# One unit of q, not two, in the first modulation's stage of a hybrid GLA and Fourier step, with two more modulation granules beside GLA and fewer on TensorE

## The chip, the cores and the metric

One core of one Trainium2 chip runs the whole kernel. The metric is the device time of one execution in microseconds (us), the median of several runs. Smaller is better.

## The reference

One layer of a diffusion backbone over 128 context tokens and 256 latent tokens (384 in all, D = 2048), everything in float32. What matters here:

```python
mod = jax.nn.silu(cond) @ lw['w_ada'] + lw['b_ada']          # D x 6D, two conditions
sh1, sc1, ga1, sh2, sc2, ga2 = jnp.split(mod, 6)
h = rmsnorm(x, norm_pre_mix) * (1.0 + sc1) + sh1
m, s_f, s_b = mixer(h, ...)                                  # proj = h @ w_in: q, k, v, gate, ...
x = x + ga1 * rmsnorm(m, norm_post_mix)
h = rmsnorm(x, norm_pre_ffn) * (1.0 + sc2) + sh2
ff = (silu(h @ w_ffn_gate) * (h @ w_ffn_up)) @ w_ffn_down
x = x + ga2 * rmsnorm(ff, norm_post_ffn)
```

The mixer runs gated linear attention (GLA, four heads, q and k of 128 columns a head, v of 256) in two directions, a two-dimensional DFT branch, and merges both with sigmoid gates of `h`.

## The kernel before

Activations lie transposed (channels on partitions, 384 tokens in the free dimension). For accuracy, each float32 operand of a large product is split into two parts of type fp32r, `hi` (a copy on ACT) and `lo` (a subtraction on DVE), and each product is three matmuls: hi·hi, hi·lo, lo·hi. Weights come in *granules* of 128x1024 (512 KB): SP issues the transfer to `raw` (L234), ACT makes `whi` (L300), DVE makes `wlo` (L287). `proj` (L348 on) computes one *unit* (128 output columns for 384 tokens): two *half units* of 24 matmuls each (L326). After each half it takes a step of the work that runs beside it, by a generator.

The stages around the change, in order of time:

**First stage** (L529 on, sixteen turns `kb` of one loop, one for each block of 128 channels). Turn `kb` makes shift and scale of block `kb` from two 1 MB slabs of `w_ada` (`gemv`, L474, 32 instructions), turns them to columns (L595), makes `h` of that block (DVE and ACT, L583 to L379), and, a turn behind, computes v of the block before it (`vprod`, L491, three times 6 matmuls) and `XU` units of q (`xprod`, L509, 3 matmuls each). The products of a turn are added to SBUF accumulators by DVE (`flush`, L504). From turn 3 the second q unit uses the PSUM bank `pgm`, which `gemv` also writes. Each turn loads one `w_v` granule (512 KB), `w_x` (128 rows of `XU`x128 floats, 128 KB here) and the two slabs, all for the turn after it. SP issues them in program order; the `raw` buffers (two) come free with DVE's `wlo` (L297). Turn 4 also loads five small tables (L457 to L461).

**GLA stage.** The other q and k units (`qk_order`), then 25 units of the merge gates (`GF`). Beside each half unit, `side` (L969) takes one step of `gla()` (L779) and one of `ada`, the modulation of the other parts. `gla()` for head 0 has some empty steps (`if h == 0: yield`). Its PE work: scores `at` (L875) need `ki` of DVE (L852) of the step before; state updates `dl` (L788) need the split of `ko` (L379, `part`) of the step before.

**Modulation granules** (`ada_rest`, L685). For m = 2, 3, 4 and two halves of 1024 columns: sixteen granules of `w_ada` (512 KB, issued by POOL, two buffers `adaw`) and then one step without work, one with PE's selection products (L718), one with the turn to columns. A granule is computed in one of two ways. On DVE: two operations of 128x1024 (L705 for the first, L707). On PE (`on_pe[0]` true): four products with the 128x32 stationary `spad` (L697), eight instructions in the trace. The last granules run beside `w_out`.

**Mix stage.** Eight `o` units (two halves each), sixteen Fourier units `b` (`four`), and sixteen `a` units (24 matmuls, L326, `pmm<-o_hi`), in `mix_order`. `side` (L1179) counts half units of `o` in `turn` and takes modulation steps there; each `a` unit in the table `TAIL` takes one step ahead of its product, on PE where the table says True. An `a` unit's product is merged by DVE (L1296, L1297) and split to `mT` (L379, `A_lo`). Then `w_out` reads `mT`.

In the trace before, PE does ten granules: at `turn` 7, 9, 11, 13, 15 and in `a` units 1, 5, 8, 11, 13.

Of the kernel before, what the change touches and what calls it, by code (L numbers as in the profile page):

```python
# [25 lines left out]
T = TC + TL  # L26
# [8 lines left out]
FC = 4  # L35
NFC = FT // FC
G = 1024
XU = 2
GF = 25
GD = 256  # L40
TAIL = {1: True, 4: False, 5: True, 8: True, 10: False, 11: True, 13: True, 14: False, 15: False}


C_TRI = 0
# [63 lines left out]
def tile_step(ctx: ExitStack, tc: tile.TileContext, a, o):  # L108
# [49 lines left out]
    srcs = [a["w_v"][k] for k in range(KT)]  # L158
    qk_order = [i for i in (4, 5, *range(XU, 4), 6, 7)]
    for i in qk_order:  # L160
# [250 lines left out]
    with ExitStack() as s:  # L411
# [11 lines left out]
        def load_w(kb):  # L423
            load()
            xraw[kb] = pb.tile([P, XU * P], F32, tag="xraw", name="xraw", bufs=2)
            SP.dma_start(xraw[kb], a["w_x"][kb])
# [39 lines left out]
        pgm = pss.tile([P, 512], F32, tag="side", name="pgm")  # L466
        pgv, pmod = pgm[:, 0:256], pgm[:, 256:512]
        px = pss.tile([P, T], F32, tag="side", name="px")
# [37 lines left out]
        def xprod(u, kb, w, bank=px):  # L506
            def mm():
                for j, (x_, w_) in enumerate(passes(w)):
                    PE.matmul(bank, w_[:, u * P : (u + 1) * P], hT[x_][:, kb, :], start=j == 0, stop=j == 2)  # L509

            return mm, lambda dst=None: flush(xacc[u], kb == 0, dst, bank)
# [38 lines left out]
        prev = None  # L550
        for kb in range(KT):
            if kb and kb + 1 < KT:
                load_slab(kb + 1)
                load_w(kb + 1)
                if kb == 4:
                    load_later()

            wait = kb in (1, 2)
            if kb and not wait:
                gemv(kb)  # L560
            todo = []
            if kb > 4 and kb % 4 == 2:
                todo.append(lrprod(kb - 6))

            both = kb > 2
            if both:
                xs = [xprod(u, kb - 1, prev[1], bank) for u, bank in enumerate((px, pgm[:, 0:T]))]
            elif kb:
                todo += [xprod(u, kb - 1, prev[1]) for u in range(XU)]
            todo += [None] * (4 - len(todo))  # L570
            flushes = [t[1] if t else lambda: None for t in todo]

            def pe_x(n):
                if todo[n]:
                    todo[n][0]()

            if wait:
                vprod(kb - 1, prev[0], (0,))
            pe_x(0)
            hf = scr[:, kb % 8, :]  # L580

            xr = hf if kb else qs[0]
            DVE.tensor_mul(xr, xn(kb), rstd if kb else px)  # L583
            flushes[0]()
            if wait:
                gemv(kb)
            if kb:
                ev = pb.tile([P, 256], F32, tag="ev", name="ev")
                ACT.copy(ev, pgv)
            lag = []  # L590
            new = split_w(kb, lag)
            if kb:
                vprod(kb - 1, prev[0], (1 if wait else 0,))
            for m in range(2):
                PE.transpose(pmod[:, m * P : (m + 1) * P], ev[:, m * P : (m + 1) * P], ident)  # L595
            if kb == 0:

                for _ in range(6):
                    PE.matmul(pv[5][:, 0:P], ones, ones, start=True, stop=True)
            pe_x(1)  # L600

            pm = pb.tile([P, 2, 2], F32, tag="pm", name="pm", bufs=2)
            DVE.tensor_reduce(
                pm, pmod.rearrange("p (m q r) -> p m r q", m=2, q=4)[:, :, 0:2, :], axis=mybir.AxisListType.X, op=ALU.add,
            )
            DVE.tensor_scalar(
                mods[:, 1, kb, :], pm[:, 1, :], bsc1[:, 0, kb : kb + 1], norms[:, 0, kb : kb + 1],
                op0=ALU.add, op1=ALU.mult,
            )
            DVE.tensor_scalar_add(mods[:, 0, kb, :], pm[:, 0, :], cols[:, 0, kb : kb + 1])  # L610
            for lo, hi, c in segs:
                DVE.tensor_scalar(
                    hf[:, lo:hi], xr[:, lo:hi], mods[:, 1, kb, c : c + 1], mods[:, 0, kb, c : c + 1],
                    op0=ALU.mult, op1=ALU.add,
                )
                if kb == 0:
                    ACT.activation(
                        hT[0][:, kb, lo:hi], xr[:, lo:hi], AF.Identity,
                        bias=mods[:, 0, kb, c : c + 1], scale=mods[:, 1, kb, c : c + 1],
                    )  # L620
            flushes[1]()
            if kb:
                split_act(hT[0][:, kb, :], hT[1][:, kb, :], hf)
            else:
                ACT.copy(rstd, px)
                DVE.tensor_sub(hT[1][:, kb, :], hf, hT[0][:, kb, :].bitcast(F32))
            if kb:
                if not wait:
                    vprod(kb - 1, prev[0], (1,))
                pe_x(2)  # L630
                flushes[2]()
            if both:
                for mm, _ in xs:
                    mm()
                for _, fl in reversed(xs):
                    fl()
            for sub in lag:
                sub()
            if kb:
                vprod(kb - 1, prev[0], (2,))  # L640
                pe_x(3)
                flushes[3]()
            prev = new
# [39 lines left out]
    on_pe = [False]  # L683
# [69 lines left out]
    with ExitStack() as s:  # L753
# [25 lines left out]
        def gla():  # L779
# [10 lines left out]
            for h in range(NH):  # L790
# [38 lines left out]
                for d in range(2):  # L829


                    bT = pss.tile([P, T], F32, tag="side", name="bT")
                    for t in range(3):
                        for j, l in enumerate((lah, lal)):
                            PE.matmul(
                                bT[:, t * P : (t + 1) * P], l[:, t, d], tri[:, d * P : (d + 1) * P],
                                start=j == 0, stop=j == 1,
                            )
                    sx = pss.tile([P, 2, P], F32, tag="side", name="sx")
                    for j, l in enumerate((lah, lal)):  # L840
                        PE.matmul(
                            sx, tri[:, (2 + d) * P : (3 + d) * P], l[:, 0 : 2 + d : 1 + d, d], start=j == 0, stop=j == 1,
                        )
                    eb = pg.tile([P, T], F32, tag=f"eb{d}", name="eb")
                    ACT.activation(eb, bT, AF.Exp)
                    ki = pg.tile([P, T], F32, tag=f"ki{d}", name="ki")
                    ACT.activation(ki, bT, AF.Exp, scale=-1.0)
                    ko = pg.tile([P, 2, P], F32, tag=f"ko{d}", name="ko")
                    ACT.activation(ko, sx, AF.Exp)
                    qi = pg.tile([P, T], F32, tag=f"qi{d}", name="qi")  # L850
                    DVE.scalar_tensor_tensor(qi, eb, DK**-0.5, qT[:, h, :], op0=ALU.mult, op1=ALU.mult)
                    DVE.tensor_mul(ki, ki, kT[:, h, :])  # L852
                    DVE.tensor_mul(ko, ko, krs[:, 0 : 2 + d : 1 + d, :])

                    last = 0 if d else CH - 1
                    tot = chunks(eb)[:, :, d, last : last + 1]
                    kc = pg.tile([P, 3, CH], F32, tag=f"kc{d}", name="kc")
                    DVE.tensor_mul(kc, chunks(ki)[:, :, d, :], tot.to_broadcast([P, 3, CH]))
                    dc = pg.tile([P, 1], F32, tag=f"dc{d}", name="dc")
                    c = 5 if d else 2  # L860
                    e0, e1 = c * CH + last, (c + 1 - 2 * d) * CH + last
                    DVE.tensor_mul(dc, eb[:, e0 : e0 + 1], eb[:, e1 : e1 + 1])
                    qin.append(qi)
                    kin.append(ki)
                    kcr.append(kc)
                    kout.append(ko)
                    dec.append((tot, dc))
                    yield

                ats = []  # L870
# [128 lines left out]
    px = fs.enter_context(tc.tile_pool(name="px", bufs=1))  # L999
# [93 lines left out]
    with ExitStack() as s:  # L1093
# [83 lines left out]
        turn = [0]  # L1177

        def side():  # L1179
            while True:  # L1180
                on_pe[0] = turn[0] > 6 and turn[0] != 8
                if turn[0] < 9 or turn[0] % 2:
                    next(ada_gen, None)
                on_pe[0] = False
                turn[0] += 1
                next(df, None)
                next(nw, None)
                yield
# [121 lines left out]
    with ExitStack() as s:  # L1310
# [94 lines left out]
        u = pd.tile([P, 2, 3], F32, name="u12", bufs=1)  # L1405
# [355 lines left out]
        bank = {}  # L1761
# [69 lines left out]
        for kind, c, i in steps[:-4]:  # L1831
# [8 lines left out]
            if kind == "D":  # L1840
# [9 lines left out]
                h = hid_last if last_c else hid  # L1850
# [248 lines left out]
```

## Time and profile before

| | |
|---|---|
| median of 3 runs | 1942.72 us (1942.26 to 1943.35) |
| the profiled execution | 1942.28 us |
| its span, first to last instruction | 1940.4 us |
| granted TensorE clock, mean | 0.998 |
| first stage, about | 0 to 142 us |
| GLA stage | 142 to 456 us |
| mix stage, `o` / `a` and `b` | 537 to 651 / 651 to 733 us |
| `w_out` | 733 to 869 us |
| FFN | 886 us to the end |

Times in the profile are microseconds from the first instruction unless marked ns. PE is TensorE's matmul, PEld its weight load, DVE VectorE, ACT ScalarE, POOL GpSimd, SP the engine that issues most transfers ("q" behind a name: its sequencer). L707 is line 707 of the kernel. A matmul's busy time overlaps with that of the next one, so the pace of PE is read from the starts of its instructions, or from the chain of waits, not from their durations.

### The profile page before, as it was taken

To read this page: it belongs to the slowest core of one execution; us is meant where nothing else is said; L and a number is where in the kernel's file an instruction comes from. 1 tells how busy PE (TensorE), PEld (TensorE's weight loads), DVE (VectorE), ACT (ScalarE), POOL (GpSimd) and SP (SyncE) were. 2 spreads that over 40 slices of the span, in tenths; PEclk is the share of its full clock that TensorE was granted. 3 is DMA by queue.
4 is the path that set the end of the run, shared out by engine and by line. 5 is a ranking of instruction groups with operands and counts; after the bars stand their busy time and mean duration, and the time that the engine had idled before them with its cause. 6 is when DMAs were issued, how large, how long until landed. Compare 5 with 4: busy or idle time off the path is not lost.

```text
span 1940.4 us, 27538 instructions
## 1 busy us (share of the span) xinstructions
PE 1920.4 (99%) x10534; PEld 1690.8 (87%) x10534; DVE 1647.8 (85%) x2172; ACT 916.3 (47%) x1298; POOL 85.8 (4%) x154
## 2 busy tenths in 40 slices
PE   9999999999999999999999999999999999999997
PEld 5779999999999999999988888888888888888886
DVE  5668898889878887978789888999998999888885
ACT  4235455545456554456455444444444444444444
POOL 0001111100000000104000000000000000000001
PEclk9999999999999999999999999999999999999999
DMA  9977766766757885755264636363636272625243
GB/s 390 387 260 248 240 234 227 248 231 194 225 185 246 302 302 181 245 193 198 83 195 131 200 103 194 121 211 98 216 104 213 91 222 93 201 76 185 87 173 110
DMA packets 200615, 380.52 MB, mean 196 GB/s; under 512 B 14196, under 2 KB 126932, under 8 KB 196132
## 3 DMA queue, kind: packets, MB, share of 16 engines
q1 hardware_dynamic: 181252, 320.84, 48.9%
q0 software_dynamic: 13952, 50.39, 8.5%
q10 hardware_dynamic: 5280, 7.55, 1.1%
q8 instruction: 82, 1.34, 0.3%
q14 instruction: 49, 0.40, 0.1%
HBM read 361.94 MB, written 16.78 MB: 195 GB/s over the span
## 4 chain that ended last, share of the span: by engine, by line
PE 93%; DVE 3%; DMA 2%; issue 1%; ACT 1%; SPq 0%; DVEq 0%; ACTq 0%
PE pgu L338 30%; PE pmm L326 30%; PE pdn L338 18%; PE pv L491 3%; PE pgm L474 1%; PE pf L1239 1%; PE pfo L1039 1%; DVE adacc L707 1%; PE pmm L1516 1%; PE ptr L1808 1%; PE pf L1240 1%; PE pfo L1040 1%; DMA xraw<-in_w_x 1%; PE po L788 1%; PE px L509 0%
## 5 line engine op out<-in xcount | busy, mean ns | idle before, releaser
L326 PE MATMUL pmm<-A_hi,whi 128*128 128x384 f32 x1072 | 361.7, 337 | 0.0
L326 PE MATMUL pmm<-A_hi,wlo 128*128 128x384 f32 x1072 | 358.8, 335 | 0.0
L326 PE MATMUL pmm<-A_lo,whi 128*128 128x384 f32 x1072 | 358.6, 335 | 0.0
L1663 ACT CAST whi<-u 128x1024 fp32r<-128x1024 f32 x200 | 210.6, 1053 | 281.5 <-DVE u L1647 86.5
L1663 ACT CAST whi<-raw 128x1024 fp32r<-128x1024 f32 x175 | 184.2, 1052 | 200.8 <-PE pgu L338 63.8
L1674 DVE TENSOR_TENSOR wlo<-u,whi 128x1024 fp32r<-128x1024 f32 x200 | 244.1, 1220 | 32.0 <-ACT whi L1663 18.3
L338 PE MATMUL pgu<-whi,A_hi 128*128 128x512 f32 x640 | 250.0, 391 | 0.0
L338 PE MATMUL pgu<-whi,A_lo 128*128 128x512 f32 x640 | 249.3, 389 | 0.0
L1674 DVE TENSOR_TENSOR wlo<-raw,whi 128x1024 fp32r<-128x1024 f32 x175 | 213.4, 1220 | 34.6 <-ACT whi L1663 25.6
L287 DVE TENSOR_TENSOR wlo<-raw,whi 128x1024 fp32r<-128x1024 f32 x163 | 198.2, 1220 | 24.1 <-ACT whi L300 23.7
L300 ACT CAST whi<-raw 128x1024 fp32r<-128x1024 f32 x149 | 156.0, 1051 | 117.6 <-PE pmm L326 50.0
L326 PEld LDWEIGHTS pmm<-A_hi,whi 128*128 128x128 f32 x1072 | 201.2, 188 | 3.3 <-issue 2.5
L326 PEld LDWEIGHTS pmm<-A_lo,whi 128*128 128x128 f32 x1072 | 201.4, 188 | 0.2
L326 PEld LDWEIGHTS pmm<-A_hi,wlo 128*128 128x128 f32 x1072 | 201.2, 188 | 0.3 <-DVE wlo L287 0.2
L707 DVE SCALAR_TENSOR_TENSOR adacc<-adaw,spad,adacc 128x1024 f32<-128x1024 f32 x160 | 198.1, 1279 | 3.5 <-DMA adaw<-in_w_ada 3.2
L338 PE MATMUL pdn<-whi,hid_hi 128*128 128x512 f32 x480 | 186.9, 389 | 0.0
L338 PE MATMUL pdn<-whi,hid_lo 128*128 128x512 f32 x480 | 186.8, 389 | 0.0
L338 PE MATMUL pgu<-wlo,A_hi 128*128 128x512 f32 x640 | 184.2, 389 | 0.0
L338 PEld LDWEIGHTS pgu<-whi,A_hi 128*128 128x128 f32 x640 | 120.2, 188 | 26.1 <-issue 0.8
L338 PEld LDWEIGHTS pgu<-wlo,A_hi 128*128 128x128 f32 x640 | 120.1, 188 | 25.4
L338 PEld LDWEIGHTS pgu<-whi,A_lo 128*128 128x128 f32 x640 | 120.1, 188 | 25.0
L338 PE MATMUL pgu<-whi,S 128*128 128x512 f32 x480 | 131.1, 395 | 0.0
(405 smaller groups left out, 3042.7 us busy)
## 6 DMA issues: line engine op xcount, KB each, us to landing
adaw<-in_w_ada POOLq DMA_DIRECT2D x96, 512.0 KB, 4.0
raw<-in_w_d SPq DMA_DIRECT2D x88, 512.0 KB, 3.7
slab<-in_w_ada SPq DMA_DIRECT2D x32, 1024.0 KB, 10.2
raw<-in_w_gate SPq DMA_DIRECT2D x64, 512.0 KB, 4.4
raw<-in_w_g SPq DMA_DIRECT2D x48, 512.0 KB, 3.4
raw<-in_w_u SPq DMA_DIRECT2D x48, 512.0 KB, 3.5
raw<-in_w_in SPq DMA_DIRECT2D x44, 512.0 KB, 4.3
u<-in_w_u SPq DMA_DIRECT2D x40, 512.0 KB, 4.6
```

Of the source, the lines that this page charges most:

```text
L287: eng.tensor_sub(lo, raw, hi.bitcast(F32))
L300: ACT.copy(hi, raw)
L326: PE.matmul(dst, w[wi][:, k * n + n0 : k * n + n0 + P], x[xi][:, k0 + k, :], start=first and k == 0 and j == 0, stop=last and k == kts - 1 ...
L338: PE.matmul(dst, stat[x_][m], mov(w[w_], m), start=first and w_ == m == x_ == 0, stop=last and w_ == m == 1,)
L474: PE.matmul(pgv[q : q + 32, :], spad[:, k, :], slab[k // (KT // 2)][:, k % (KT // 2), :], start=k < 4, stop=k >= KT - 4,)
L491: PE.matmul(pv[2 * t + g], hT[x_][:, kb, t * P : (t + 1) * P], w_[:, g * 512 : (g + 1) * 512], start=kb == 0 and j == 0, stop=kb == KT - 1 ...
L707: DVE.scalar_tensor_tensor(acc[:, c, :], w, spad[:, k, c : c + 1], acc[:, c, :], op0=ALU.mult, op1=ALU.add,)
L788: PE.matmul(dst, w[wi], x[xi], start=first and j == 0, stop=last and j == 2)
L1039: PE.matmul(p, w_of[0][:, i, k, g, :], x[:, :, lo:hi], start=kt == 0, stop=False)
L1040: PE.matmul(p[:, 0], w_of[1][:, i, k, g, :], x[:, 0, lo:hi], start=False, stop=kt == KT - 1)
L1663: ACT.copy(hi, src)
L1674: DVE.tensor_sub(lo, src, hi.bitcast(F32))
```

## The change

```diff
-XU = 2
+XU = 1
 GF = 25
 GD = 256
-TAIL = {1: True, 4: False, 5: True, 8: True, 10: False, 11: True, 13: True, 14: False, 15: False}
+TAIL = {4: False, 8: False, 10: False, 11: False, 13: False, 14: False, 15: False}
...
             if both:
-                xs = [xprod(u, kb - 1, prev[1], bank) for u, bank in enumerate((px, pgm[:, 0:T]))]
+                xs = [xprod(u, kb - 1, prev[1], bank) for u, bank in enumerate((px, pgm[:, 0:T])[:XU])]
...
                     dec.append((tot, dc))
+                    yield
+                if h == 0:
                     yield
...
         def side():
             while True:
-                on_pe[0] = turn[0] > 6 and turn[0] != 8
+                on_pe[0] = turn[0] > 8
                 if turn[0] < 9 or turn[0] % 2:
                     next(ada_gen, None)
```

- The first stage computes unit 0 of q alone. `w_x` is 64 KB a turn, and `pgm` is no longer used for q.
- Unit 1 of q becomes an ordinary unit of the GLA stage (`qk_order` is 4, 5, 1, 2, 3, 6, 7). Its two half units take two steps of `ada`, both granules on DVE, and two of `gla()`.
- Head 0 of `gla()` has one more empty step, between the decays of the second direction and the scores.
- The `a` units take seven modulation steps, not nine, and none of them on PE; `turn` 7 takes its granule on DVE.
- Counted through, PE does granules at `turn` 9, 11, 13 and 15 alone, four in place of ten, and DVE 92 in place of 86. From `w_out` on both kernels take the same steps.

## The prediction

> **What bounds the kernel now.** I read the page first, then the chain of waits, then the stages that the change touches.
>
> ```profile
> PE 1920.4 (99%) x10534; PEld 1690.8 (87%) x10534; DVE 1647.8 (85%) x2172; ACT 916.3 (47%) x1298; POOL 85.8 (4%) x154
> PE 93%; DVE 3%; DMA 2%; issue 1%; ACT 1%; SPq 0%; DVEq 0%; ACTq 0%
> ```
>
> The chain that ends last runs over PE for 93% of the span. So an instruction taken from PE's stream is worth its pace, unless another engine or a transfer then comes last. DVE (85%) and the transfers are the candidates, each in its own stage.
>
> In the first stage the chain of one turn, in order of time (start, us, what), is this; the two rows on top are from turn 1:
>
> ```profile
> 28.03 0.52 ACT A_hi L378
> 28.57 0.56 DVE A_lo L379
> ...
> 105.65 1.86 PE pgm L474 x32
> 107.52 1.59 PE pv L491 x6
> 109.10 0.22 PE pgm L595 x2
> 109.32 1.39 PE pv L491 x6
> 110.71 0.52 PE px L509 x3
> 111.23 0.52 PE pgm L509 x3
> 111.75 1.39 PE pv L491 x6
> 113.14 1.86 PE pgm L474 x32
> ```
>
> PE works through, 113.14 - 105.65 = 7.49 us a turn, and 0.52 us of it are the second q unit (the row `pgm L509`). Turn 1 alone hangs on ACT and DVE. The transfers are close behind, though. The windows' last two columns are the DMA engines' busy share and GB/s; the later rows are the issue of a pair of slabs and their use in the timeline, the landing times of the slabs issued between 90 and 135 us, SP's longest wait, and, for 44 to 62 us, the weight load that waited for a slab:
>
> ```profile
> 30.00:40.00 10.00, 9.78 (x92) 6.17 (x91) 5.86 (x14) 3.29 (x6) 0.00 (x0) 1.00 1.03 416
> 60.00:80.00 20.00, 20.00 (x163) 14.25 (x156) 12.07 (x31) 6.00 (x11) 0.00 (x0) 1.00 1.02 415
> 100.00:110.00 10.00, 10.00 (x74) 7.52 (x71) 5.23 (x14) 3.76 (x7) 0.00 (x0) 1.00 0.96 334
> 110.00:120.00 10.00, 10.00 (x72) 7.68 (x71) 6.58 (x17) 2.65 (x5) 0.00 (x0) 1.00 0.98 363
> ...
> 99.92 0.86 SPq L419 DMA_DIRECT2D slab<-in_w_ada  x2
> 113.08 1.93 PE L474 MATMUL pgm<-slab,spad 128*32 128x256 f32 x32
> ...
> DMA to landing us min/median/max: 9.2/9.9/10.6
> ...
> SPq L234 <- DVE wlo L297: 84.9, 15, 7.2
> ...
>   PEld pgm L474: 0.3, 1
> ```
>
> A turn moves 2 x 1.049 + 0.524 + 0.131 = 2.75 MB. At 415 GB/s that is 6.6 us, under PE's 7.49. SP waits 84.9 us for DVE to free the `raw` buffers, so the loop paces the transfers, not they the loop. Late in the stage the slabs land at 99.92 + 9.9 = 109.8 and are used at 113.08, 3.3 us later. But around turn 6, after SP was held up by the five small tables, a weight load of PE's did wait 0.3 us for a slab: there the margin is gone already.
>
> **The change part by part.**
>
> *The q unit leaves the first stage.* Sixteen products of 0.52 us leave. That of turn 1 gains nothing (ACT and DVE come last there); the others give 15 x 0.52 = 7.8 us. Turn 2 had one wait for the split of `w_x`,
>
> ```profile
> 30.66 0.44 PE L509 MATMUL px<-A_hi,wlo 128*128 128x384 f32 x1 [0.22 <-DVE wlo L440]
> ```
>
> and half that width saves some 0.1 us. Against it stands turn 6. PE gets there 4 x 0.52 = 2.1 us earlier, while the slab comes earlier only by the bytes saved: six half `w_x`, 0.39 MB at 416 GB/s, 0.9 us. The missing 1.2 us become a wait (bounds: 0, as the slot waits of SP may move too; 2.1 if the slab does not move at all). Later turns need 2.69 MB / 415 = 6.5 us against 6.97 and fall back behind PE. Sum: 7.8 + 0.1 - 1.2 = **-6.7** us.
>
> *It comes back as two half units in the GLA stage.* The chain has a pair of half units there as
>
> ```profile
> 242.50 8.32 PE pmm L326 x48
> ```
>
> **+8.3** us. The 1 MB of granules that it loads falls where the DMA engines are 70% busy; its DVE work is below.
>
> *PE granules.* Ten become four. The mix stage shows the price, as its groups of three `a` units with and without a PE granule stand side by side (first column: length in us; third: DVE busy):
>
> ```profile
> 658.08:670.67 12.59, 12.59 (x77) 12.59 (x73) 10.78 (x20) 6.03 (x10) 0.53 (x1) 1.00 0.98 369
> 673.05:686.37 13.32, 13.32 (x82) 12.66 (x81) 12.41 (x21) 6.41 (x11) 1.04 (x2) 1.00 0.91 312
> 688.75:702.08 13.33, 13.33 (x82) 12.67 (x81) 10.21 (x19) 6.42 (x11) 0.53 (x1) 1.00 0.87 296
> 704.46:717.79 13.33, 13.33 (x83) 12.67 (x81) 12.42 (x21) 6.41 (x11) 1.05 (x2) 1.00 0.82 289
> 720.83:750.15 29.32, 29.32 (x172) 29.07 (x168) 22.75 (x31) 13.26 (x20) 2.11 (x4) 1.00 0.69 233
> ...
> 677.35 0.64 PE L697 MATMUL pr<-adaw,spad 128*32 128x256 f32 x8
> ```
>
> 13.32 - 12.59 = 0.73 us for each of `a` 5, 8 and 11 (the instructions and the change of form around them). The three others (`turn` 7, `a` 1, `a` 13) stand next to other small products; I take 0.66. Sum: 3 x 0.73 + 3 x 0.66 = **-4.2** us (bounds: 6 x 0.57 = 3.4 from the granule's first instruction to the next, 677.35 to 677.92; 6 x 0.73 = 4.4).
>
> *The wait in head 0 of GLA.* This is the one place after the first stage where the chain leaves PE for DVE:
>
> ```profile
> 178.97 1.22 DVE L287 TENSOR_TENSOR wlo<-raw,whi 128x1024 fp32r<-128x1024 f32 x1
> 180.10 2.47 DVE L707 SCALAR_TENSOR_TENSOR adacc<-adaw,spad,adacc 128x1024 f32<-128x1024 f32 x2
> 182.49 1.21 DVE L287 TENSOR_TENSOR wlo<-raw,whi 128x1024 fp32r<-128x1024 f32 x1
> ...
> 191.34 0.57 PE L875 MATMUL at<-qi,ki 128*64 128x64 f32 x12
> ...
> 193.46 0.57 PE L875 MATMUL at<-qi,ki 128*64 128x64 f32 x12 [1.55 <-DVE ki L852]
> ...
> 210.49 0.75 DVE L379 TENSOR_TENSOR part<-ko,part 128x256 fp32r<-128x256 f32 x2
> 211.22 0.88 PE L788 MATMUL dl<-vr,part 128*128 128x256 f32 x6
> ```
>
> DVE is full from 152 us and behind: the second half of `at` waits, some 1.7 us in PE's pace. The added empty step puts `at` one half unit (4.2 us) later, past `ki`. What is late next is `dl`. An empty step still costs DVE a weight split and a granule, 182.49 - 178.97 = 3.5 us. The first `part` is ready at 210.49 + 0.4 and moves to 214.4; PE, without the old wait, reaches `dl` at 211.22 - 1.7 + 4.2 = 213.7. So about 0.8 us of the wait return there: **-0.9** us (bounds: -1.7, all gone; 0, all moved). Behind `dl` stand only more half units. The two steps of `ada` without DVE work follow directly, so DVE catches up.
>
> *DVE in the mix stage.* Granules of 2.4 us are new on DVE at `turn` 7 and at `a` 8, 11 and 13. From 658 us on DVE has 1.8, 0.9, 3.1 and 0.9 us free in the four groups above, and some 1.5 of the 6.6 free in the last window lie ahead of `a` 14 (an estimate); PE gets 3.5 us faster up to `w_out`. DVE's last split for `w_out` is now
>
> ```profile
> 736.47 1.23 DVE L379 TENSOR_TENSOR A_lo<-yb,A_hi 128x384 fp32r<-128x384 f32 x2
> ```
>
> and ends at 737.7. The granules at `a` 8, 11 and 13 add 7.2 us, of which the free time up to there (0.9 + 3.1 + 0.9 + 1.5) takes 6.4: some 738.5. `w_out`'s second half ends at 720.83 + 29.32 x 5/7 = 741.8 now and reads that split 0.4 us before its end, 3.5 us earlier after the change: 737.9. The two meet within what this working can tell. I cost it at **0**, as PE's earlier products let DVE start earlier too; it is up to 0.7 if they don't.
>
> Sum: -6.7 + 8.3 - 4.2 - 0.9 = -3.5. On the profiled execution's 1942.28 (span 1940.4 and 1.9 around it) that is **1938.8**; this execution lies 0.4 under the median 1942.72, so the result should show as 0.2% less.
>
> The Trainium skill speaks against this, in "DMA: Bandwidth & Descriptors", section "Where 436 GB/s comes from": from HBM to SBUF the HBM side binds at about 358 GB/s. By that rule a turn's 2.69 MB would take 7.5 us and the first stage would give nothing. The trace's 416 and 415 GB/s differ from it, its 334 and 363 do not; rival two takes it up.
>
> **The rivals.**
>
> 1. *More is hidden.* SP's slot waits move with the loop, turn 6 costs nothing, and the whole wait of head 0 goes: -7.9 + 8.3 - 4.2 - 1.7 = -5.5, **1936.8**. For it: SP waits mostly for DVE. Against it: the 0.3 us wait at turn 6.
> 2. *The transfers set the first stage* (the slower side). If they can't go under today's 7.49 us a turn, the 6.7 are lost and the unit comes back all the same: +8.3 - 4.2 - 0.9 = +3.2, **1945.5**; at the 334 GB/s of 100 to 110 us a turn takes 2.69 / 0.334 = 8.0, and five such turns add 2 to 3 us, 1948. It decides from the point where a turn's transfers take over 6.97 us, 385 GB/s. For it: a DMA share near 1.0 through the stage, and the two late windows. Against it: PE's unbroken chain, SP's 84.9 us, and 3.3 us of margin when the rate is low, where few transfers are out.
> 3. *DVE sets the mix stage.* If half of the three new granules of 2.4 us at `a` 8, 11, 13 comes through as waits, +3.6: **1942.4**; if all does, 1946. For it: `w_out` behind it is nearly full of DVE work too. Against it: the free time in the windows.
>
> That the change does not do what it says: its words speak of seven granules, the flags make six; that is in the sum.
>
> **How the numbers follow.** A measurement of this kernel can tell about 0.2% from no change, 3.9 us: under 1938.8 of the median is faster, over 1946.6 slower. The forecast has 0.5, with its own range 1937.0 to 1940.5, and it lies on the bound: 0.27 faster, 0.23 within. Rival one 0.22, faster. Rival two 0.2, of which 0.11 slower and 0.09 within. Rival three 0.08, within but for 0.02. So faster 0.49, within 0.38, slower 0.13. The range, 1935.5 to 1945.8, leaves out half of rival two, part of three and the far end of one.
>
> **What would show it.** In the first stage a turn of 6.97 us from one `gemv` to the next and no `pgm L509`; one wait for a slab of about 1.2 us near turn 6, and v done some 6.7 us earlier. In GLA no wait at `at`, and one under 1 us at `dl`. In the mix stage groups of three `a` units of 12.6 us throughout, 32 of L697 instead of 80, and no PE wait where `w_out` begins. I am wrong if a turn stays near 7.5 us with `gemv` behind slabs (rival two), or if PE waits for DVE between 690 and 745 us (rival three).

## The result and the profile after

| | before | after |
|---|---|---|
| median of the runs beside each other | 1942.26 us (22 runs, 1941.17 to 1944.93) | 1944.90 us (22 runs, 1943.27 to 1949.79) |
| the profiled execution | 1942.28 us | 1943.9 us |
| its span | 1940.4 us | 1942.1 us |

The ratio after / before is 1.0016, with an interval of 1.0010 to 1.0022. The change made the kernel some 2.6 us slower, where a gain of 3.5 was forecast. The profiled execution of after is 1.0 us faster than its median, that of before is at its median; so the traces hold 1.7 us of the 2.6.

The page of after, busy times and the shares of the chain that ended last:

```profile
PE 1917.0 (99%) x10486; PEld 1689.3 (87%) x10486; DVE 1653.2 (85%) x2170; ACT 915.8 (47%) x1301; POOL 85.8 (4%) x154
PE 85%; DVE 7%; DMA 4%; ACT 2%; issue 2%; SPq 0%; DVEq 0%; ACTq 0%
```

PE has 3.4 us less work than before, as the granules have gone, and yet the span is longer. The chain has less of PE (85%, not 93%) and more of DVE (7%, not 3%) and of transfers (4%, not 2%): PE waits where it did not wait. The list of PE's waits up to 760 us says where (what waited for what: us in total, times, longest; left out are four lines of the first stage, the largest of which, 4.2 us, before has as well):

```profile
PE dl L788 <- DVE part L379: 1.5, 1, 1.5
PE pf L1242 <- DVE wlo L287: 1.5, 2, 0.8
PE pf L1241 <- ACT whi L294: 1.2, 1, 1.2
PE pgm L474 <- DMA slab<-in_w_ada: 1.0, 3, 0.6
PE bT L835 <- DVE lal L379: 0.4, 1, 0.4
PE pmm L326 <- DVE A_lo L379: 0.3, 1, 0.3
```

(Lines from 869 on stand two lower than in the kernel before: L1242 is its L1240.) Set side by side, the starts of the same half units (24 products of L326 each) in the two traces give the account. Each line is what the distance grew by in that stretch; a wait is counted as what a product starts later than at its usual pace, which is a little more than the list's idle time (`dl` has 1.5 in the list and 1.69 here):

| stretch | after - before | what it is |
|---|---|---|
| first stage, to 135 us | -7.05 | turns of 6.97 us; 0.76 and 0.47 of waits for slabs, turns 3 and 6 |
| the pair of half units | +8.32 | unit 1 of q |
| rest of GLA, to 564 us | +0.9 | 1.74 before `at` goes; 1.69 before `dl`, 0.48 before `bT` and small ones come |
| `o` and `a` units, to 720 us | -0.9 | three waits in the `b` units between the `o`, 3.25; six granules less, 6 x 0.66; 0.2 is not accounted for |
| start of `w_out` | +0.7 | wait for the split of its input |
| after 945 us | -0.3 | |
| span | +1.7 | |

The new turn of the first stage in the chain of waits (start, us, what):

```profile
95.90 0.22 PE pgm L474 x4
96.12 1.58 PE pv L491 x6
97.70 0.22 PE pgm L595 x2
97.92 1.39 PE pv L491 x6
99.31 0.52 PE px L509 x3
99.84 1.39 PE pv L491 x6
101.23 1.86 PE pgm L474 x32
```

`pgm L509` is gone and PE still works through. In head 0 the chain leaves PE; this is its way into DVE's full stretch in after, with the long pieces of both sides, and from the timelines of after and of before the first weight split there (idle time before it and who ended it in brackets):

```profile
133.35 4.82 DMA raw<-in_a
138.19 6.38 DMA raw<-in_w_in
149.44 5.18 DMA raw<-in_w_in
...
191.28 2.47 DVE adacc L707 x2
```
```profile
145.73 1.23 DVE L287 TENSOR_TENSOR wlo<-raw,whi 128x1024 fp32r<-128x1024 f32 x1 [5.87 <-ACT whi L300]
```
```profile
152.33 1.23 DVE L287 TENSOR_TENSOR wlo<-raw,whi 128x1024 fp32r<-128x1024 f32 x1 [4.42 <-ACT whi L300]
```

DVE does not begin its full stretch when PE ends the first stage, but when a weight block has landed, and that was issued behind small loads (`in_a`). PE came to the GLA stage 7.05 us earlier, DVE 6.60.

The mix stage, DVE's timeline of after around `turn` 7:

```profile
588.57 2.47 DVE L707 SCALAR_TENSOR_TENSOR adacc<-adaw,spad,adacc 128x1024 f32<-128x1024 f32 x2
...
595.76 0.68 DVE L244 TENSOR_TENSOR ws<-raw 128x512 f32<-128x512 f32 x1
596.36 2.47 DVE L707 SCALAR_TENSOR_TENSOR adacc<-adaw,spad,adacc 128x1024 f32<-128x1024 f32 x2
598.75 0.61 DVE L1201 SCALAR_TENSOR_TENSOR gs<-gs,gnorm,pt 128x384 f32<-128x384 f32 x1
...
600.89 1.23 DVE L287 TENSOR_TENSOR wlo<-ws,whi 128x1024 fp32r<-128x1024 f32 x1 [0.39 <-ACT whi L294]
602.03 1.22 DVE L287 TENSOR_TENSOR wlo<-raw,whi 128x1024 fp32r<-128x1024 f32 x1
```

and ACT's, a little later:

```profile
599.40 0.51 ACT L378 CAST o_hi<-gs 128x384 fp32r<-128x384 f32 x1 [4.73 <-DVE gs L1201]
599.82 1.04 ACT L294 CAST whi<-ws 128x1024 fp32r<-128x1024 f32 x1
```

The second granule, that of `turn` 7, stands ahead of the `o` unit's own work on DVE (`gs`, L1201). ACT idles 4.73 us for that, and its copy `whi` of the next weight block stands behind `o_hi` in its stream. `pf L1241` waits for this `whi`, and `pf L1242` for the split `wlo` that DVE makes from it. The windows (length; PE, PEld, DVE, ACT, POOL busy) of after and then of before:

```profile
590.00:605.00 15.00, 12.99 (x81) 12.38 (x80) 13.89 (x25) 7.99 (x13) 1.06 (x2) 1.00 0.66 211
605.00:620.00 15.00, 14.31 (x93) 13.19 (x92) 13.89 (x27) 9.30 (x14) 1.05 (x2) 1.00 0.73 260
```
```profile
590.00:605.00 15.00, 15.00 (x102) 14.11 (x104) 13.73 (x31) 9.35 (x15) 1.05 (x2) 1.00 0.80 251
605.00:620.00 15.00, 15.00 (x105) 13.96 (x98) 12.63 (x26) 10.07 (x15) 0.53 (x1) 1.00 0.80 250
```

DVE has 1.1 us free in 15 in each stretch of after, in before 1.3 and 2.4; PE loses 2.0 and 0.7 us. The busy share alone does not decide it: in e6 below, which has the granule of `turn` 7 on PE, DVE is busy for 13.88 us of the first stretch, as long as here, and PE for all 15. What decides is what the granule stands ahead of.

### The profile page after: what moved, and what is told of

The parts are those of the page before. It is cut to its first block, busy times and chain, and to the rows that moved or that the text cites. A ratio compares the mean times of both kernels' runs of the same rounds, so it can differ in the third digit from the quotient of the medians.

```text
span 1942.1 us, 27457 instructions
## 1 busy us (share of the span) xinstructions
PE 1917.0 (99%) x10486; PEld 1689.3 (87%) x10486; DVE 1653.2 (85%) x2170; ACT 915.8 (47%) x1301; POOL 85.8 (4%) x154
## 4 chain that ended last, share of the span: by engine, by line
PE 85%; DVE 7%; DMA 4%; ACT 2%; issue 2%; SPq 0%; DVEq 0%; ACTq 0%
PE pgu L338 31%; PE pmm L326 25%; PE pdn L338 18%; PE pv L491 2%; DMA slab<-in_w_ada 2%; DVE adacc L707 2%; DVE wlo L287 2%; PE pfo L1041 1%; PE pgm L474 1%; PE pmm L1518 1%; DMA raw<-in_w_in 1%; PE pf L1241 1%; PE ptr L1810 1%; PE pfo L1042 1%; PE po L788 1%
## 5 line engine op out<-in xcount | busy, mean ns | idle before, releaser
L326 PE MATMUL pmm<-A_hi,whi 128*128 128x384 f32 x1088 | 366.9, 337 | 0.0
L326 PE MATMUL pmm<-A_lo,whi 128*128 128x384 f32 x1088 | 364.2, 335 | 0.3 <-DVE A_lo L379 0.3
L326 PE MATMUL pmm<-A_hi,wlo 128*128 128x384 f32 x1088 | 364.1, 335 | 0.1
L707 DVE SCALAR_TENSOR_TENSOR adacc<-adaw,spad,adacc 128x1024 f32<-128x1024 f32 x172 | 212.9, 1280 | 2.2 <-DMA adaw<-in_w_ada 1.9
L326 PEld LDWEIGHTS pmm<-A_hi,whi 128*128 128x128 f32 x1088 | 204.2, 188 | 3.3 <-issue 2.5
L326 PEld LDWEIGHTS pmm<-A_lo,whi 128*128 128x128 f32 x1088 | 204.4, 188 | 1.0 <-DVE A_lo L379 0.8
L326 PEld LDWEIGHTS pmm<-A_hi,wlo 128*128 128x128 f32 x1088 | 204.2, 188 | 0.5 <-DVE wlo L287 0.4
```

Of the source, the lines that this page charges most:

```text
L326: PE.matmul(dst, w[wi][:, k * n + n0 : k * n + n0 + P], x[xi][:, k0 + k, :], start=first and k == 0 and j == 0, stop=last and k == kts - 1 ...
L707: DVE.scalar_tensor_tensor(acc[:, c, :], w, spad[:, k, c : c + 1], acc[:, c, :], op0=ALU.mult, op1=ALU.add,)
```

## The experiments

Each was run in turn with the kernel before, 9 to 11 runs of it against 15 to 33. The column "against before" is the difference of the two medians; the intervals of the ratios are about 0.002 wide, some 3.5 us, so two rows less than some 2 us apart are not told apart by their times alone, and the traces decide.

| run | what | against before, us | ratio, interval |
|---|---|---|---|
| after | the change | +2.6 | 1.0010 to 1.0022 |
| e1 | unit alone | +5.1 | 1.0011 to 1.0031 |
| e2 | step alone | +1.6 | 0.9998 to 1.0016 |
| e12 | unit and step | +3.8 | 1.0012 to 1.0031 |
| e5 | flags and table alone | -1.5 | 0.9980 to 0.9997 |
| e11 | flags, nine late granules | +1.1 | 0.9996 to 1.0014 |
| e13 | flags, faster steps in `w_out` | -3.6 | 0.9971 to 0.9989 |
| e3 | after, turns 5 to 7 on PE | +2.4 | 1.0006 to 1.0024 |
| e6 | after, turn 7 on PE | +0.3 | 0.9992 to 1.0010 |
| e7 | after, two steps skipped | +0.4 | 0.9994 to 1.0012 |
| e4 | after, tables at turn 11 | +2.1 | 1.0001 to 1.0019 |
| e8 | after, small loads on POOL | +1.8 | 0.9999 to 1.0017 |
| e9 | e5 and e8 together | -1.2 | 0.9986 to 1.0004 |
| e10 | after with e4, e6, e8 | +0.4 | 0.9992 to 1.0009 |

**e1, the unit alone.** The kernel before with

```diff
-XU = 2
+XU = 1
-                xs = [xprod(...) for u, bank in enumerate((px, pgm[:, 0:T]))]
+                xs = [xprod(...) for u, bank in enumerate((px, pgm[:, 0:T])[:XU])]
```

> The kernel before with one unit of q in the first stage and nothing else: no empty step in head 0, the old table of late steps, ten granules on TensorE. My theory (the first stage gives 7, the unit costs 8.3 in GLA, and the two extra GLA steps shift the modulation's steps so that granules of turns 5 and 6 keep VectorE from serving the o units): -7.0 + 8.3 + 0.1 with the wait of head 0 where it was (1.7 us at `at`), + about 2.4 of waits in the o units of turns 5 and 6 (599 to 601 us in the kernel after), none at turn 7, no gain from granules: +3.7 against before, 1946. Rival one, the granules taken off TensorE in the late a units are what made VectorE late, the o units are not shifted into a wait: +1.4, 1943.7. Rival two, the transfers of the first stage make it slower in most executions than in the one profiled: 1 us more than either, with times spread over 3 us and more.

Measured: 1947.70 us against 1942.58. Its waits of PE, cut to the lines that matter:

```profile
PE at L875 <- DVE ki L852: 2.3, 1, 2.3
PE pgm L474 <- DMA slab<-in_w_ada: 1.5, 2, 0.8
PE pmm L326 <- DVE wlo L287: 1.1, 1, 1.1
PE pf L1240 <- DVE wlo L287: 0.3, 1, 0.3
```

My theory had turns 5 and 6 as the cause of the waits in the `o` units; they take their granules on DVE here too, and `pf` waits 0.3 us, not 2.7. So that theory fell: `turn` 7 is needed. The wait of head 0 is longer than before, 2.3 for 1.5 us: with PE earlier and DVE tied to its transfer the unit costs there as well. The 1.1 us of `pmm L326` are at 525 us: DVE idled 2.87 us there for a weight block, in after 0.68 us for the same one. That wait belongs to the execution: after, e3, e4 and e10 have none there, e6 and e12 have 0.6 and 1.5.

**e2, the step alone.** The kernel before with

```diff
+                if h == 0:
+                    yield
```

> The kernel before with the empty step before `at` in head 0 and nothing else. My theory: VectorE is full from 145 us on and an empty half unit brings it a split and a granule as any other, so the wait only moves: no wait at `at`, 1.7 us at `dl`, time within 0.4 us of before. The prediction's working: half of it goes, -0.9. Rival: all of it goes, -1.7, and the wait at `dl` in the kernel after belongs to the unit of q.

Measured: 1944.21 us. Its waits of PE:

```profile
PE pmm L326 <- DVE wlo L287: 1.5, 1, 1.5
PE bT L835 <- DVE lal L379: 0.4, 1, 0.4
...
PE dl L788 <- DVE part L379: 0.2, 1, 0.2
```

In its own place the step did what the prediction said: `at` waits no more and `dl` 0.2 us. The price comes some 250 us later, at 459.51, which none of the three named. DVE's timeline there, of this run and then of before:

```profile
442.21 3.25 DVE L948 TENSOR_SCALAR qk<-qk,rs 128x256 f32<-128x256 f32 x12
```
```profile
442.17 2.19 DVE L946 TENSOR_SCALAR qk<-qk,rs 128x256 f32<-128x256 f32 x8
```

GLA takes one step a half unit, and there are just enough half units. One step more pushes a piece of its last work (four scalings more in one go) behind the last half unit, ahead of DVE's work for the next stage. In the change the unit's two half units make room for it.

**e12, unit and step.** Both edits of e1 and e2 together.

> The kernel before with one unit of q in the first stage and the step before `at`, and the old flags and table (ten granules on TensorE): against the run with the unit alone the step's worth where the unit is there, against the kernel after the worth of the flags. Theory: the wait of 2.5 us at `at` becomes one of 0.5 to 1.7 at `dl` and 0.5 at `bT`, -1 to -1.5 against the unit alone; and the flags are worth 6 x 0.66 - 2.8 (o units) - 0.5 (w_out) = 0.7, so 0.7 above the kernel after: 1945.6 to 1946.5. Rival (the step costs 1.5, as it did with two units, by the GLA steps that it pushes behind the last half unit): 1949.

Measured: 1946.09 us against 1942.31, which is where the theory put it. By the times alone e1 and e12 are not told apart, though, and the trace shows no gain from the step: e12's profiled execution (1947.92 us, 1.8 above its median) waits 1.8 us at `dl`, 0.4 at `bT` and 1.5 at 526 us, that of e1 2.3 at `at` and 1.1 at 525 us. So the step's worth beside the unit is not shown. `pf` waits 0.3. By the medians the flags of the change are worth 1.2 on top.

**e5, the flags alone.** The kernel before with

```diff
-TAIL = {1: True, 4: False, 5: True, 8: True, 10: False, 11: True, 13: True, 14: False, 15: False}
+TAIL = {4: False, 8: False, 10: False, 11: False, 13: False, 14: False, 15: False}
-                on_pe[0] = turn[0] > 6 and turn[0] != 8
+                on_pe[0] = turn[0] > 8
```

> The kernel before with two units of q in the first stage and no added step: only the flags and the table of late steps are those of the kernel after (four granules on TensorE, not ten; turn 7's on VectorE, with the end of the third block). Theory one (the waits in the o units come from a row of VectorE granules in turns 5 to 8, which only the shift by two steps together with turn 7's flag makes): here turns 5 and 6 have no granule, so under 0.5 us of wait in the o units, -6 x 0.66 = -4.0, and up to 0.7 at w_out: -3.3 to -4 against before. Theory two (turn 7's granule alone is enough): 3 us of waits in the o units as in the kernel after: -0.3 to -1.

Measured: 1941.15 us against 1942.65, faster than both kernels. Theory one holds for the `o` units: `turn` 7's granule is on DVE, and `pf` waits 0.3 us. But more than half of the 4.0 is missing from the median. The waits of PE between 760 and 900 us and, from PE's timeline, the place:

```profile
PE pr L718 <- DVE adacc L707: 1.0, 2, 0.6
PE ptm L671 <- ACT adev L667: 0.5, 1, 0.5
```
```profile
838.17 0.34 PE L326 MATMUL pmm<-A_hi,wlo 128*128 128x384 f32 x1
839.08 0.64 PE L718 MATMUL pr<-adacc,selr 128*32 128x256 f32 x8 [0.57 <-DVE adacc L707]
840.19 0.64 PE L718 MATMUL pr<-adacc,selr 128*32 128x256 f32 x8 [0.47 <-DVE adacc L707]
841.32 0.44 PE L671 MATMUL ptm<-ident,adev 128*128 128x128 f32 x2 [0.49 <-ACT adev L667]
```

The table has seven late steps and not nine, and here no half units of q take the other two, so the last block's end is run in one piece at unit 12 of `w_out`, with no products between. Against the usual pace that is 2.4 us.

**e11, the flags with all nine steps.** e5 with

```diff
+TAIL = {1: False, 4: False, 5: False, 8: False, 10: False, 11: False, 13: False, 14: False, 15: False}
```

> Two units of q in the first stage and no added step; four granules on TensorE as in the kernel after, and the table of late steps with all nine entries, those of a 1 and a 5 on VectorE too. In the run with the flags alone two steps were missing, and the last block's end came in one piece at 838 to 841 us, where TensorE waited for VectorE and ScalarE between its own products (0.74 + 0.84 + 0.86 us over the usual pace). Theory (those 2.4 us are the price of the two steps that the q unit's half units bring in the kernel after; VectorE has room for two granules more around a 1 and a 5): -6 x 0.66 = -4.0 against before, +0.4 in the o units, +0.5 to 1.2 at w_out, no such waits: -2.4 to -3.1, so 1939.5, and 1.5 below the run with the flags alone. Rival (nine granules are too many for VectorE between a 1 and w_out): 1.5 us and more of waits for VectorE between 690 and 745 us, no gain over the run with the flags alone.

Measured: 1943.41 us. The rival holds. Its waits of PE between 640 and 760 us, and the window of 700 to 720 us:

```profile
PE pf L1240 <- DVE wlo L287: 3.1, 2, 1.6
PE pmm L326 <- DVE A_lo L379: 1.1, 1, 1.1
```
```profile
700.00:720.00 20.00, 18.41 (x112) 18.09 (x111) 19.79 (x32) 8.00 (x15) 1.05 (x2) 1.00 0.87 287
```

Seven granules fit between a 4 and a 15, nine between a 1 and a 15 do not: DVE is busy for 19.79 of 20 us.

**e13, the two steps made up in `w_out`.** e5 with

```diff
-        rate[0] = 0.85
+        rate[0] = 0.95
```

> Two units of q in the first stage, no added step, flags and table of the kernel after (seven late steps), and in w_out's stage modulation steps at a rate of 0.95 a half unit, not 0.85, which makes up for the two steps that the q unit's half units take in the kernel after. Theory (the run with the flags alone lost 2.4 us where the last block's end came in one piece at 838 to 841 us, and nine late granules were too many): that piece is gone and VectorE takes the two steps between 750 and 840 us without a wait: 2.4 us below the run with the flags alone, 1938.5 to 1939, the fastest of all. Rival (VectorE is as full in w_out's stage, 45 of 50 us between 750 and 800, and the two steps come back as waits there): 1941 as the run with the flags alone, with waits for VectorE between 745 and 860 us.

Measured: 1938.93 us against 1942.51, the fastest of all. Of the piece at 838 us one wait is left:

```profile
836.87 0.64 PE L718 MATMUL pr<-adacc,selr 128*32 128x256 f32 x8 [0.20 <-DVE adacc L707]
```

So six granules off TensorE are worth about what was forecast, when they come without the shift and the two missing steps are made up: 3.6 of the 4.0.

**e6 and e3, granules of after back on PE.** e6 takes `turn` 7 alone, e3 turns 5, 6 and 7:

```diff
-                on_pe[0] = turn[0] > 8
+                on_pe[0] = turn[0] > 6 and turn[0] != 8
```
```diff
+                on_pe[0] = turn[0] > 4 and turn[0] != 8
```

> The kernel after with the granule of turn 7 back on TensorE (five there). Theory (turn 7's granule fills the row; turns 5 and 6 alone do little, as the run with the unit alone has 0.43 us there): +0.66 for the granule, the waits of 1.36, 1.06 and 0.83 us go but for 0.4: -2.2 against after. Rival (the granules of turns 5 and 6 are enough for it): half of the waits stay, -0.7 or less.

> The kernel after with the granules of turns 5, 6 and 7 on TensorE (seven there, not four). My theory: three granules cost TensorE 3 x 0.66 = 2.0, the three waits in the o units (1.36 + 1.06 + 0.83 = 3.25) go: -1.3 against after. Rival one, those waits come from the b units' own work on VectorE and ScalarE and stay whatever the granules: +2.0 against after. Rival two, they fold into the later waits (VectorE is behind all the way to w_out): -1.3 in the o units but the 0.7 at w_out grows, near 0 in all.

Measured: e6 1942.95 us, e3 1945.01. e6 is as the theory said: it lies 2.3 us lower against before than after does, for the 2.2 worked out, and `pf` waits

```profile
PE pf L1242 <- DVE wlo L287: 0.3, 1, 0.3
```

Its trace is 1.4 us ahead of that of after at 945 us. A first stage that is 0.4 us later and 0.7 us at the weight block of 524 us, of which after's execution has nothing, are the most of what is missing there.

In e3 no `pf` waits at all, and up to 945 us its trace is 2.1 us ahead of that of after, a microsecond of it from a shorter wait at `dl`. The median shows nothing of that. In its profiled execution the lead is lost at 1888 us, where ACT's timeline has

```profile
1887.61 1.05 ACT L1665 CAST whi<-raw 128x1024 fp32r<-128x1024 f32 x1 [3.92 <-DMA raw<-in_w_d]
```

against 2.18 us of waiting for the same block in before and after. It is a late transfer in the FFN. e7 has it too, with 3.34 us; why these have it and others not I can't say, so e3 is a miss that stays open.

**e7, two steps skipped in head 0.** After, with a 1 and a 5 on PE again and

```diff
-                next(ada, None)
+                if nth[0] not in (4, 5):
+                    next(ada, None)
+                nth[0] += 1
```

> The kernel after with no modulation step in the two empty half units of head 0 of GLA, so that two granules of 2.47 us leave VectorE's full stretch, and all later steps stand again where they stood before the change; a 1 and a 5 take the two steps that are left over, on TensorE as in the kernel before (six granules there). Theory (VectorE's granules make the wait in head 0, and the shift by two makes those in the o units): no wait at `dl` (-1.7), none over 0.5 us in the o units (-2.8), +2 x 0.66 for TensorE: -3.2 against after. Rival one (turn 7's granule alone makes the o waits): -0.4. Rival two (the wait in head 0 hangs on the transfer that starts VectorE at 145.7 us, and VectorE has other work enough): `dl` keeps 1 us or more.

Measured: 1943.02 us, 2.3 us lower against before than after, not 3.2. Both waits went as the theory said, `dl` to none and `pf` to 0.3. Its trace has 2.4 of the 3.2 at 945 us; 0.8 went to the weight block at 522.6 us. Behind 945 us it loses another 1.5 against after, where the late transfer is.

**e8, the small loads on another queue.** After with `SP.dma_start(raw3...)` as `POOL.dma_start(raw3...)`, four places, ten transfers.

> The kernel after with the ten small loads for GLA (constants and the decay weights, lines 763 to 771) issued by GpSimd's queue, not SP's. In the kernel after SP issues a weight block behind them at 138.2 us, it lands at 144.6, and VectorE, idle for 5.9 us until 145.7, is full from there to 208. Theory (the wait in head 0 is set by that late start): the block is issued some 3 to 5 us earlier, VectorE starts 2 us or more earlier, the wait of 1.7 us at `dl` goes, -1.5 to -2 against after with those in the o units unchanged. Rival (the transfers are full there, or the granules come later instead): VectorE starts as late, 0.

Measured: 1944.41 us. The start of DVE's stretch in its timeline:

```profile
142.21 2.36 DVE L287 TENSOR_TENSOR wlo<-raw,whi 128x1024 fp32r<-128x1024 f32 x2 [3.64 <-ACT whi L300]
```

DVE starts 3.5 us earlier than in after and `dl` waits no more; `bT` waits 0.7 us, in after 0.4. DVE's late start is the cause of the wait in head 0. The other traces bear it out: the time from PE's first half unit to the start of DVE's full stretch differs between executions, and the wait, in PE's pace, rises with it.

| wait at | run | DVE's start after PE's, us | wait, us |
|---|---|---|---|
| `at` | e5, e11, e13 | 8.75, 8.90, 9.14 | 0.45, 0.61, 0.87 |
| `at` | before, e1 | 10.03, 10.32 | 1.74, 2.52 |
| `dl` | e8, e10 | 6.48, 6.59 | none |
| `dl` | e2, e3 | 9.59, 9.89 | 0.34, 0.67 |
| `dl` | e6, after, e4, e12 | 10.36, 10.47, 10.53, 10.66 | 1.49, 1.69, 1.73, 1.93 |

e9 alone is out of line, with 6.48 and still 0.50 at `at`; e7, which skips two granules there, is not in the table. Of the 1.7 us the median shows 0.9 (+1.8 for +2.6). In the trace 1.1 of the 1.7 are taken up by longer waits for slabs, for `bT` and at 523 us, and it is 0.6 ahead of that of after at 945 us.

**e4, the tables later.** After, with four of the five small loads of the first stage at its turn 11.

> The kernel after with four of the five small tables loaded at turn 11 of the first stage, not at turn 4. Theory one (the tables delay the slab of turn 6): the wait there, some 0.5 us, goes, that of turn 3 (0.75) stays: -0.5 against after. Theory two (the waits for slabs in the first stage also cost the clock of later work, and they make the times of after spread over 3 us): -1 or more in the median, with a spread like that of before. Rival (any table moved only moves the wait, the transfers have no margin in any turn): 0, with a wait near turn 12 or 13.

Measured: 1944.72 us. Its waits for slabs are

```profile
PE pgm L476 <- DMA slab<-in_w_ada: 0.5, 1, 0.5
```

that of turn 3 alone, and turn 6 waits no more: theory one. The median lies 0.5 us lower against before than that of after, which is as worked out but within the noise. The runs lie between 1943.28 and 1945.61, narrower than those of after, but there are 11 for 22.

**e9 and e10, together.** e9 is e5 with the loads of e8; e10 is after with e4, e6 and e8.

> Two units of q in the first stage, as before; the flags and late steps of the kernel after; the ten small loads for GLA on GpSimd's queue. Theory (the three findings add up): no wait at `at` (1.74 us in the profiled execution of before, 0.45 in that of the run with the flags alone), -4.0 for six granules, 0.4 in the o units and 0.5 at w_out: -4 to -5 against before, 1938 to 1939. Rival (the run with the flags alone has that wait's gain already, by chance or not): as that run, 1941.

> One unit of q in the first stage with every mend that the runs showed: the kernel after with turn 7's granule on TensorE, the ten small loads for GLA on GpSimd's queue, and four of the five tables of the first stage at its turn 11. Theory (with the waits gone what is left of the change is the exchange, 8.32 of a pair of half units against 7.05 and the 0.5 us of the tables): slower than the other kernel of this pair by 8.3 - 7.6 + 0.66 for one granule more on TensorE = 1.4 us, that is 1939.5 to 1940.5, and faster than before by 2 to 3 us. Rival (one unit in the first stage costs the clock or the transfers more than the profiled executions show): 1 us or more above that, and a spread over 3 us.

Measured: e9 1940.97 us, e10 1942.63. e9 is no faster than e5, as its rival said: with two units in the first stage `at` idles 0.3 us with and without the other queue. It has e5's 2.4 us too, at 840 us. e10 lies 1.7 us above e9, as the theory's 1.4, but 2 to 3 above the time named: up to 945 us its trace is 4.3 us ahead of after's, as worked out, and 1.8 of it are lost in two waits at 1886 and 1888 us. With these waits mended the kernel with one unit is still no faster than before.

## Why the prediction was wrong

It had the right list of terms, and two of them with the wrong size; both are times of DVE.

1. **The first stage, -6.7: right.** -7.05 in after; in the six other traces with one unit and the tables at turn 4 it ends 6.1 to 6.9 us earlier than in before. A turn is 6.97 us, and turn 6 waits. But that the sum came out is in part luck: the prediction had 1.2 us of wait at turn 6, where the trace has 0.47, and none at turn 3, where it has 0.76 (0.58 of it idle time of PE, in the second half):

```profile
37.41 1.07 PE L474 MATMUL pgm<-slab,spad 128*32 128x256 f32 x16 [0.58 <-DMA slab<-in_w_ada]
58.85 1.07 PE L474 MATMUL pgm<-slab,spad 128*32 128x256 f32 x16 [0.29 <-DMA slab<-in_w_ada]
```

   Rival two fell. The window of 60 to 100 us has 403 GB/s:

```profile
60.00:100.00 40.00, 40.00 (x310) 28.31 (x303) 22.89 (x58) 12.28 (x24) 0.00 (x0) 1.00 1.01 403
```

   By the Trainium skill's "DMA: Bandwidth & Descriptors", "Where 436 GB/s comes from" (about 358 GB/s from HBM), an estimate for a turn is 7.5 us, as the prediction has it; this trace, with 403 GB/s and 6.97 us, does not agree.

2. **The unit, +8.3: right**, 8.32.

3. **The granules, -4.2: right within its bounds**, 0.66 each, -4.0.

4. **"The wait in head 0", -0.9: failed.** After has 1.69 + 0.48 us of waits for the 1.74 of before, +0.4. The step of the reasoning that failed is "PE, without the old wait, reaches `dl` at 211.22 - 1.7 + 4.2" against a `part` that "moves to 214.4": it moved both by the added step and took for granted that the 7 us of the first stage move PE and DVE alike. They don't. DVE's stretch starts with a transfer, and came 6.60 us earlier for PE's 7.05 (6.1 for 6.4 in e1); e8 moved that start, and the wait went. In e2, where the first stage is that of before, 0.34 at `dl` and 0.48 at `bT` came back, near the 0.8 worked out. (214.4 - 213.7 is 0.7, not 0.8; it changes nothing.) Besides, the 1.74 was the wait of one execution: with the same code up to there `at` starts 0.45, 0.61 and 0.87 late in e5, e11 and e13. Less was to be had than the trace of before showed.

5. **"DVE in the mix stage", 0: failed, by 3.9.** 3.25 us in the `o` units and 0.7 at `w_out`. The prediction names the new granule at `turn` 7 and then adds up DVE's free time only "from 658 us on", behind all `o` units; `turn` 7's 2.47 us were never placed. Nor was the other half: two more half units in GLA mean that all later modulation steps come two earlier, so the two steps without DVE work move from turns 5 and 6 to 3 and 4, and granules come to 5 and 6, where the `b` units load DVE. Neither alone does it: without `turn` 7 (e1, e6, e12) or without the shift (e5, e7, e13) `pf` waits 0.3 us. A row of four granules, turns 5 to 8, does: after, e4 and e8 have it, and `pf` waits 2.7 us in all three. Where the prediction did look, its sum was good: at `w_out` it had "up to 0.7".

6. **Rival three** (DVE sets the mix stage) was the mechanism, at another place; that its price of 3.6, for half of three other granules, is near the 3.9 is chance. The place that it named, the late `a` units, comes to be bound with two granules more: e11 shows it.

By the runs' medians: unit and step, e12, +3.8 (forecast -6.7 + 8.3 - 0.9 = +0.7), flags, e13, -3.6 (forecast -4.2), together +0.2; after has +2.6, and the 2.4 between fit the two acting together in the `o` units, of which e6 takes 2.3 back with one granule. The 3.1 that e12 lies over its forecast are not all explained: its one trace has 0.6 more in the first stage, 1.6 more in head 0 and 1.6 at 526 us, but that execution lies 1.8 above the median.

Not settled: the 1.0 us by which after's median lies above its profiled execution, and why its runs reach up to 1949.79 us. The longest have a lower mean granted clock (0.995 in that one, 0.998 in the profiled one), which is about the 0.3% by which they are longer; no trace shows where the clock was lost.

## What to carry to other kernels

A list of work that is consumed one step at a time has a phase: whoever adds or removes a slot early moves every later step, and must lay the whole new list beside the stages' loads, each granule by its place. A gain ahead of a stage moves the engine that was the bound; the others start with whatever starts them, here a weight block queued behind ten small loads. And a wait that is to be removed is looked at in more than one execution first.

## What had not been expected of the hardware

A wait of the same code differs by more than a microsecond between executions: `at` starts 0.45 to 1.74 us late, with a start of DVE's stretch 8.75 to 10.03 us behind PE's; and ACT's wait for one weight block late in the FFN is 2.15 us in e9 and 3.92 in e3. And one piece of DVE's work can cost PE all of its length where PE waits for what comes behind it: the granule of `turn` 7 takes 2.47 us on DVE, and with it on PE, at 0.66 us, the 3.25 us of waits fell to 0.4 and the median by 2.3.
